# Moving the build of a bias table to the end of the mLSTM, and shorter norm steps for two token blocks, in a two-layer encoder step

## The chip, the cores and the metric

The kernel runs on one core of one Trainium2 chip. The metric is the device time of one execution in microseconds (us), a median over runs. The engines are called as in the profile: PE is TensorE's matrix multiply and PEld its weight load, DVE is VectorE, ACT is ScalarE, POOL is GpSimd, SP is the engine from whose queue nearly all DMAs of this kernel are issued.

## The reference, cut to what matters

The step has two layers over 1024 prompt tokens and 32 sample tokens, 1024 features, all in float32. Layer 0 mixes with an mLSTM, layer 1 with a chunk-band attention that adds a learned bias per head and clipped distance. Each layer ends in a squared-ReLU MLP of width 4096, and each of the four sublayers ends in a LayerNorm.

```python
def trunk(x, ...):
    for l in range(DEPTH):
        sh1, sc1, g1, sh2, sc2, g2 = jnp.split(ada_mod(c, p['w_ada'][l], p['b_ada'][l])[:, None, :], 6, axis=-1)
        u = x * (1 + sc1) + sh1
        ...  # y = mlstm_mixer(u) in layer 0, band attention with rel_bias(table) and @ w_out_b in layer 1
        x = layer_norm(ALPHA * x + (1 + g1) * y, p['ln_g'][l, 0], p['ln_b'][l, 0])
        u = x * (1 + sc2) + sh2
        f = jnp.square(jax.nn.relu(u @ p['w_up'][l])) @ p['w_down'][l]
        x = layer_norm(ALPHA * x + (1 + g2) * f, p['ln_g'][l, 1], p['ln_b'][l, 1])

def rel_bias(table, q_off, tq, tk):            # table: 16 heads x 257 distances
    rel = q_off + jnp.arange(tq)[:, None] - jnp.arange(tk)[None, :]
    idx = jnp.clip(rel, -MAX_REL, MAX_REL) + MAX_REL
    return table[:, idx].astype(jnp.float32)
```

## The kernel before, in words

Features lie on the partitions (8 chunks of 128), tokens along the free axis. The tokens are handled in three blocks, `TBS`: block 0 and block 1 have 384 tokens, block 2 has 288. Every float32 product is three passes of a rounded format (lines 118 to 120: high part times high part, high times low, low times high), so a weight tile is first loaded raw, then rounded to a high part on ACT (line 89) and the rest taken on DVE (line 90). Raw tiles live in a ring of three buffers under the tag `raw`, split weights in a ring of six under the tag `wc`.

The stages come one after the other: mLSTM of layer 0 with its output gates (`o_proj`), its output projection (`op_a`), the up product of layer 0, its down product (`dn_plain`, eight groups g of four weight tiles `w_dn`; the last group goes block by block), the query and key products, the attention, the output projection of layer 1 (`op_b`), and the up and down products of layer 1.

Side work is cut into generators and handed to a `Flow` object. The main loops call `flow.tick(us)`; each tick lowers the waiting time of every task, and a task whose time has run out runs on to its next `yield`, whose value is its next waiting time. So a tick's number places side work between units of matrix work in program order. The framework then orders the instructions of each engine from that program order and its own estimates, before anything runs; on the chip each engine goes through its list in order. Only where `tc.manual_schedule` stands is PE's order taken as written.

Two pieces of side work matter here.

`bias_table` builds in DRAM (`bias_d`, 16 x 64 x 576) the bias that the attention will read: it loads the table (`tab`), turns it on ACT and DVE into one row per head (`rev`), writes that to DRAM (`e_d`), and from there a DMA with a stride of -1 writes the 64 shifted copies. Both tiles, `tab` and `rev`, are taken from the ring `raw`. It is called at the end of `ada_rest`, the task that runs under the down product of layer 0. Its reader is at lines 1784 and 1788, at the start of the attention.

`norm` is the LayerNorm of one token block. Its steps are: the sum over features (`s_n`, split into `sr_n`), a wait `w[0]`, the mean by two matmuls with a matrix of 1/1024 (`mean_n`), the squares (`q_n`, split into `qr_n`), a wait `w[1]`, the variance by two matmuls (`var_n`), then the scaling and the modulated input of the next product (`u`, features in four pairs of chunks with waits `w[2]` to `w[4]` between them), then the gain and shift. In layer 1's output projection the blocks come in the order 2, 1, 0, and `end_out1(ti)` starts the norm of block `ti` when its last feature chunk has been added. One feature chunk of one block, called a unit here, is 24 matmuls, and ends with `flow.tick(n / 96)`, which is 4.0 for a block of 384 tokens.

```python
    W10 = ((10.0, 12.0, 0.0, 0.0, 0.0, 3.0), (16.0, 14.0, 0.0, 0.0, 0.0, 3.0))
    ...
        norms[ti] = flow.add(norm(ti, 2, f"n10_{ti}", W10[ti == rev[-1]], True, ...), now=NOW)
```

With this, blocks 2 and 1 have waits of 10 and 12, block 0 of 16 and 14.

Of the kernel before, what the change touches and what calls it, by code (L numbers as in the profile page):

```python
# [75 lines left out]
def trunk_kernel(ctx: ExitStack, tc: tile.TileContext, a, o):  # L76
    nc = tc.nc
    flow = Flow()
# [5 lines left out]
    def raw_tile(shape, name):  # L84
        return ring.tile(shape, F32, tag="raw", name=name, bufs=3)
# [71 lines left out]
    def lng(i):  # L157
        return pt1[:, i * KC:(i + 1) * KC]

    def lnb(i):  # L160
        return pt1[:, 32 + i * KC:32 + (i + 1) * KC]
# [3 lines left out]
    def ada_part(l, i):  # L165
        return ada[:, l * 48 + i * KC:l * 48 + (i + 1) * KC, :]
# [10 lines left out]
    def tpt(name):  # L177
        return pa.tile([P, 512], F32, tag="tp", name=name, bufs=2)
# [129 lines left out]
    def ada_fix(base, parts):  # L308

        for i, kind in parts:  # L310
            ap = ada[:, base + i * KC:base + (i + 1) * KC, :]
            if kind == "sc":
                nc.vector.tensor_scalar_add(ap, ap, 1.0)
            else:
                nc.vector.tensor_scalar(ap, ap, 1.0, 1.0 / ALPHA, op0=ALU.add, op1=ALU.mult)

    def combine(ni, g, b, sc, sh):

        for cnd in range(2):
            nc.vector.tensor_mul(comb[:, ni, :, 0, cnd], g, sc[:, :, cnd])  # L320
            nc.vector.tensor_mul(comb[:, ni, :, 1, cnd], b, sc[:, :, cnd])
            nc.vector.tensor_add(comb[:, ni, :, 1, cnd], comb[:, ni, :, 1, cnd], sh[:, :, cnd])
# [22 lines left out]

    def bias_table():

        tab = raw_tile([16, 257], "tab")
        nc.sync.dma_start(tab, a["rel_bias_b"][0])
        rev = raw_tile([16, 640], "rev")  # L350
        nc.vector.memset(rev[:, 639:640], 0.0)
        nc.scalar.activation(rev[:, 0:447], tab[:, 256:257].broadcast_to([16, 447]), AF.Copy, scale=8.0)
        fwd = tab[:, 65:257]
        nc.vector.tensor_scalar(rev[:, 447:639], bass.AP(fwd.tensor, fwd.offset + 191, [fwd.ap[0], [-1, 192]]),
                                8.0, None, op0=ALU.mult)
        nc.sync.dma_start(e_d, rev)

        nc.sync.dma_start(bias_d, bass.AP(e_d.tensor, e_d.offset + 63, [[640, 16], [-1, 64], [1, 576]]))


# [28 lines left out]
    def y4_tile(shape, name):  # L389
        return A.tile(shape, F32, tag="y", name=name, bufs=4)  # L390
# [420 lines left out]
    def out_rows():  # L811
        ps = tpt("tails_ps")
        nc.tensor.transpose(ps[:48, :P], tails.rearrange("p j f -> p (j f)"), ident)
        tr = A.tile([P, 256], F32, tag="hn", name="tails_r", bufs=2)[:48, :P]
        nc.vector.tensor_copy(tr, ps[:48, :P])
        nc.sync.dma_start(o["conv_p"].rearrange("l b j (k p) -> (l b j k) p", p=P), tr[0:24])
        nc.sync.dma_start(o["conv_s"].rearrange("l b j (k p) -> (l b j k) p", p=P), tr[24:48])
        ps = tpt("ncol_ps")
        nc.tensor.transpose(ps[:8, :P], ncol, ident)
        nr = A.tile([P, 256], F32, tag="hn", name="ncol_r", bufs=2)[:8, :P]  # L820
        nc.vector.tensor_copy(nr, ps[:8, :P])
        nc.sync.dma_start(o["n_p"][0, 0], nr[0:4])
        nc.sync.dma_start(o["n_s"][0, 0], nr[4:8])
        yield
    flow.add(out_rows())
    units = [0]

    def split_heads(t0, n):
# [39 lines left out]
    def acc_dma(d, x, out=False):  # L868
        for i in range(0, KC, 4):
            p = [d[:, i:i + 4], x[:, i:i + 4]]  # L870
            nc.sync.dma_start(*(p if out else reversed(p)))
# [9 lines left out]
    TAIL = (1.0, 1.5)  # L881
    W00 = (6.0, 12.0, 0.0, 0.0, 0.0, 3.0)
    W01 = ((4.0, 6.0, 1.0, 1.0, 1.0), (6.0, 8.0, 2.0, 2.0, 2.0), (3.0, 6.0, 0.0, 0.0, 0.0))
    W10 = ((10.0, 12.0, 0.0, 0.0, 0.0, 3.0), (16.0, 14.0, 0.0, 0.0, 0.0, 3.0))

    def make_layer(acc, pp, uo, cut=None):

# [654 lines left out]
    fwd, rev = (0, 1, 2), (2, 1, 0)  # L1542
# [10 lines left out]
    mm, norm, _, out_proj, _, add_gated_at = make_layer(acc, bank, uap)  # L1553
    combine(0, lng(0), lnb(0), ada_part(0, 4), ada_part(0, 3))
    norms = {}
# [26 lines left out]
    def ada_rest():  # L1582
        yield from ada_wide(a["w_ada"][1], 0, 48, 48, mm, tmp_t, wc_tile, ADA_W)
        yield from ada_wide(a["w_ada_kv"], D, 104, 8, mm, tmp_t, wc_tile, ADA_W)
        ada_fix(48, [(1, "sc"), (2, "g"), (4, "sc"), (5, "g")])
        ada_fix(96, [(1, "sc")])
        combine(1, lng(1), lnb(1), ada_part(1, 1), ada_part(1, 0))
        combine(2, lng(2), lnb(2), ada_part(1, 4), ada_part(1, 3))
        yield
        bias_table()  # L1590

    class L0:
        wups = wup0
# [41 lines left out]
        def down():  # L1635
            flow.finish(norms["ada"])
            norms["ada"] = flow.add(ada_rest(), carry=True)
# [323 lines left out]
    def open_u2(pr):  # L1961
        u2_cm.append(tc.tile_pool(name=f"u2p{pr}", bufs=1, side="right", reuse_waits="tile"))
        u2p[pr] = u2_cm[-1].__enter__()
        u2[pr] = u2p[pr].tile([P, 2, KC, 2 * QN], F32R, tag="u2", name=f"u2_{pr}")

    def u2ap(hl, k, t0, n):
# [5 lines left out]
    mm, norm, norm_out, out_proj, gain_shift, add_gated_at = make_layer(  # L1972
        acc, lambda name: psD.tile([P, 512], F32, tag="mm", name=name, bufs=8), u2ap, 2 * QN)
# [6 lines left out]

    def end_out1(ti):
        t0, n = TBS[ti]
        norms[ti] = flow.add(norm(ti, 2, f"n10_{ti}", W10[ti == rev[-1]], True, lambda ti: acc_dma(
            xsp[2][:, :, t0:t0 + n], acc[ti], True)), now=NOW)
        qo_cm[ti].__exit__(None, None, None)
        if ti == 1:
            open_u2(0)
# [6 lines left out]
    def early_up(ti, pr):  # L1994

        if ti == rev[-1] and pr:
            wup1[FIRST[pr - 1]] = up_weights(1, FIRST[pr - 1])
    out_proj([(0,), (1, 2, 3)], rev, wo_get, o_mov, ada_part(1, 2), end_out1, "b", width=[384, 384, 320],
             after_pr=early_up)

# [96 lines left out]
```

## Time and profile before

| what | value |
|---|---|
| median of 3 runs | 2437.98 us (2436.84 to 2437.99) |
| the profiled execution | 2433.89 us, of which the span is 2432.1 us |
| mean granted clock of TensorE | 0.993 |
| PE busy | 97% of the span |
| DVE busy | 81% |
| ACT busy | 48% |
| DMA moved | 423.60 MB |

The span is the time from the first to the last instruction of the profiled execution. Rows of a timeline have the start, the duration, the engine, the line and the operation as out<-in; a bracket at the end says how long the engine sat idle before it and what ended that. Rows of a table of stretches have, for each engine, its busy time and number of instructions, then the granted clock of TensorE (1.00 is full), the share of the DMA engines that was busy, and GB/s.

### The profile page before, as it was taken

The page shows a single profiled execution, that of the slowest core. Times are in us where ns is not written, and L with a number is a line of the kernel's source. Part 1 is how long each engine was busy: PE and PEld are TensorE (multiplying, and loading weights), DVE is VectorE, ACT ScalarE, POOL GpSimd, SP SyncE. Part 2 cuts the span into 40 slices and gives each one's busy share as a digit, 9 for nine tenths or more (in the row PEclk, how much of TensorE's full clock was granted, in tenths as well). Part 3 has the DMA queues.
Part 4 walks back from the last instruction along what each step waited for, and adds up shares of the span by engine and source line. Part 5 has one row for each costly group of instructions (what it writes and reads, how often), then busy time and mean ns, then how long its engine had stood idle before and what let it go on. Part 6 is the DMA issues. An engine that isn't in the chain of part 4 may idle for free.

```text
span 2432.1 us, 44293 instructions
## 1 busy us (share of the span) xinstructions
PE 2361.3 (97%) x17180; PEld 2265.0 (93%) x17180; DVE 1973.5 (81%) x4094; ACT 1179.6 (48%) x2394; POOL 166.8 (7%) x315
## 2 busy tenths in 40 slices
PE   7999999999999999999999989999999999899997
PEld 4999999999999999999989977889999999899997
DVE  4898997778788789999697666755998888887778
ACT  4654456377666620010157566763776777222212
POOL 0211100000000000000001134420000000000003
PEclk9999999999999999999999999999999999999999
DMA  8433323436556897656423220051486779966642
GB/s 296 122 112 96 101 88 99 143 114 219 179 188 192 294 346 265 234 203 231 145 67 95 74 64 1 15 135 32 163 282 229 256 259 339 364 243 232 227 151 72
DMA packets 283702, 423.60 MB, mean 174 GB/s; under 512 B 15320, under 2 KB 205164, under 8 KB 278372
## 3 DMA queue, kind: packets, MB, share of 16 engines
q1 hardware_dynamic: 279460, 390.50, 48.1%
q10 hardware_dynamic: 4032, 30.28, 3.1%
q8 instruction: 135, 2.21, 0.4%
q14 instruction: 75, 0.61, 0.1%
HBM read 304.91 MB, written 118.17 MB: 174 GB/s over the span
## 4 chain that ended last, share of the span: by engine, by line
PE 48%; DVE 12%; ACT 4%; DMA 3%; issue 2%; POOL 0%; SPq 0%; DVEq 0%; ACTq 0%; POOLq 0%
PE dn L1421 11%; PE up L1286 8%; PE dn L120 5%; PE dn L119 5%; PE dn L118 5%; PE pv L1859 3%; PE s L1802 2%; PE pt L1837 2%; DVE wf_u L90 1%; DVE HL L90 1%; DMA rdn_u<-in_w_up_dram 1%; PE op_b L118 1%; PE op_b L119 1%; PE op_b L120 1%; PE q L119 1%
## 5 line engine op out<-in xcount | busy, mean ns | idle before, releaser
L1051 DVE SCALAR_TENSOR_TENSOR ACX<-dn,ada,ACX 128x264 f32<-128x264 f32 (+6 forms) x664 | 281.8, 447 | 87.9 <-PE dn L1421 42.5
L1421 PE MATMUL dn<-fx,wf_d 128*128 128x264 f32 x2016 | 255.3, 286 | 6.0 <-DVE ACX L1051 3.7
L1421 PEld LDWEIGHTS dn<-fx,wf_d 128*128 128x128 f32 x2016 | 250.2, 189 | 8.1 <-DVE ACX L1051 2.3
L89 ACT CAST w_dn<-raw_dn 128x1024 fp32r<-128x1024 f32 x36 | 37.7, 1051 | 282.8 <-DVE aw L277 159.5
L118 PE MATMUL dn<-hs,w_dn 128*128 128x384 f32 (+2 forms) x512 | 161.3, 315 | 0.8 <-DVE ACX L1051 0.7
L119 PE MATMUL dn<-hs,w_dn 128*128 128x384 f32 (+2 forms) x512 | 160.9, 315 | 0.0
L120 PE MATMUL dn<-hs,w_dn 128*128 128x384 f32 (+2 forms) x512 | 155.9, 314 | 1.8 <-DVE w_dn L90 1.8
L1286 PE MATMUL up<-TF,wf_u 128*128 128x264 f32 x1056 | 143.4, 285 | 3.0 <-ACT H L1289 3.0
L1286 PE MATMUL up<-U,wf_u 128*128 128x264 f32 x1056 | 139.6, 285 | 1.5 <-DVE H L1292 1.1
L1286 PE MATMUL up<-u,wf_u 128*128 128x264 f32 x1056 | 139.7, 285 | 1.2 <-ACT wf_u L89 0.6
L277 DVE SCALAR_TENSOR_TENSOR aw<-radw,cs,aw 128x512 f32<-128x512 f32 x196 | 139.5, 744 | 0.0
L1286 PEld LDWEIGHTS up<-TF,wf_u 128*128 128x128 f32 x1056 | 134.3, 188 | 4.1 <-ACT H L1289 4.0
L1286 PEld LDWEIGHTS up<-U,wf_u 128*128 128x128 f32 x1056 | 133.0, 188 | 2.6 <-DVE H L1292 1.9
L1286 PEld LDWEIGHTS up<-u,wf_u 128*128 128x128 f32 x1056 | 132.6, 188 | 2.2 <-ACT wf_u L89 0.8
L119 PE MATMUL dn<-U,w_dn 128*128 128x384 f32 (+2 forms) x416 | 129.8, 313 | 0.0
L118 PE MATMUL dn<-U,w_dn 128*128 128x384 f32 (+2 forms) x416 | 129.3, 311 | 0.0
L120 PE MATMUL dn<-U,w_dn 128*128 128x384 f32 (+2 forms) x416 | 125.5, 312 | 0.6 <-DVE w_dn L90 0.6
L120 PEld LDWEIGHTS dn<-hs,w_dn 128*128 128x128 f32 x512 | 95.8, 188 | 2.9 <-DVE w_dn L90 2.6
L118 PEld LDWEIGHTS dn<-hs,w_dn 128*128 128x128 f32 x512 | 96.4, 188 | 1.4 <-DVE ACX L1051 1.0
L119 PEld LDWEIGHTS dn<-hs,w_dn 128*128 128x128 f32 x512 | 96.4, 188 | 0.0
L1812 DVE CUSTOM_DVE_ANT_0 p<-s,bias 128x576 f32<-128x576 f32 (+9 forms) x132 | 79.0, 606 | 19.6 <-PE s L1802 12.8
L90 DVE TENSOR_TENSOR HL<-H,HL 128x1056 fp32r<-128x1056 f32 x64 | 80.2, 1254 | 17.5 <-ACT HL L89 17.4
(394 smaller groups left out, 7163.4 us busy)
## 6 DMA issues: line engine op xcount, KB each, us to landing
hpl<-HL SPq DMA_DIRECT2D x144, 264.0 KB
rdn_u<-in_w_up_dram SPq DMA_DIRECT2D x64, 512.0 KB
hd<-HL SPq DMA_DIRECT2D x28, 1056.0 KB
fx<-hd SPq DMA_DIRECT2D x50, 528.0 KB
radw<-in_w_ada_dram SPq DMA_DIRECT2D x24, 1024.0 KB
hd<-HM SPq DMA_DIRECT2D x28, 792.0 KB
raw_up<-in_w_up_dram SPq DMA_DIRECT2D x40, 512.0 KB
raw_dn<-in_w_down_dram SPq DMA_DIRECT2D x36, 512.0 KB
```

The lines of the kernel that those rows point to most:

```text
L90: (eng or nc.vector).tensor_sub(dst_l, src, dst_h.bitcast(F32))
L118: nc.tensor.matmul(ps, wh, mov(0, k), start=(k == 0), stop=False)
L119: nc.tensor.matmul(ps, wh, mov(1, k), start=False, stop=False)
L120: nc.tensor.matmul(ps, wl, mov(0, k), start=False, stop=(k == nk - 1))
L277: nc.vector.scalar_tensor_tensor(acc[cnd], raw[:, k], sc, acc[cnd], op0=ALU.mult, op1=ALU.add)
L1051: nc.vector.scalar_tensor_tensor(xs, ps[:, off + o:off + o + mm_], gate[:, fc, cnd:cnd + 1], xs, op0=ALU.mult, op1=ALU.add)
L1286: nc.tensor.matmul(p, self.ws[w][:, wl, k], moving(f, tp, xl, k), start=first and k + n_ == 0, stop=k == 3 and n_ == 2, skip_group_check=n ...
L1421: nc.tensor.matmul(p, ws[w][:, wl, k], t[:, s0, xl], start=first and k + n_ == 0, stop=k == kg - 1 and n_ == 2, skip_group_check=not first)
L1802: nc.tensor.matmul(s[:, b, :w], qst, kk[i][:, g, k0 + j0:k0 + j0 + w], start=(i == 0), stop=(i == 1))
L1812: nc.vector.tensor_tensor_reduce(out=z.rearrange("p (b w) -> p b w", b=np_), in0=s[:, :np_, :w], in1=bt.rearrange("p (b w) -> p b w", b=np ...
L1837: nc.tensor.transpose(pt[:kp, j - j0, pr * P:(pr + 1) * P], ps_[pr][:, j * P:j * P + kp], ident)
L1859: nc.tensor.matmul(pv[64 * e:64 * e + 64, :nq], V[:kp, vt0 + j, g * 64:(g + 1) * 64], pts[e][:kp, j, :nq], start=(j == 0), stop=(j == nt - 1))
```

## The change

`bias_table` becomes a generator with one `yield` ahead of its last DMA. Its two tiles come from the tag `y` of the mLSTM's own pool (four buffers) instead of the ring `raw`. It is handed to the flow right behind `out_rows`, at the start of the output gates of heads 2 and 3, the last stage of the mLSTM. The call at the end of `ada_rest` is gone. The waits of the norm in layer 1's output projection get a row for each block: block 0 keeps 16 and 14, block 1 gets 9 and 10, block 2 gets 6 and 8.

```diff
     def bias_table():
-        tab = raw_tile([16, 257], "tab")
+        tab = y4_tile([16, 257], "tab")
         nc.sync.dma_start(tab, a["rel_bias_b"][0])
-        rev = raw_tile([16, 640], "rev")
+        rev = y4_tile([16, 640], "rev")
...
         nc.sync.dma_start(e_d, rev)

+        yield
         nc.sync.dma_start(bias_d, bass.AP(e_d.tensor, e_d.offset + 63, [[640, 16], [-1, 64], [1, 576]]))
...
     flow.add(out_rows())
+    flow.add(bias_table())
...
-    W10 = ((10.0, 12.0, 0.0, 0.0, 0.0, 3.0), (16.0, 14.0, 0.0, 0.0, 0.0, 3.0))
+    W10 = ((16.0, 14.0, 0.0, 0.0, 0.0, 3.0), (9.0, 10.0, 0.0, 0.0, 0.0, 3.0), (6.0, 8.0, 0.0, 0.0, 0.0, 3.0))
...
         combine(2, lng(2), lnb(2), ada_part(1, 4), ada_part(1, 3))
-        yield
-        bias_table()
...
-        norms[ti] = flow.add(norm(ti, 2, f"n10_{ti}", W10[ti == rev[-1]], True, lambda ti: acc_dma(
+        norms[ti] = flow.add(norm(ti, 2, f"n10_{ti}", W10[ti], True, lambda ti: acc_dma(
             xsp[2][:, :, t0:t0 + n], acc[ti], True)), now=NOW)
```

## The prediction

> **What bounds the kernel.** I read the engine rows of the page first, then the table of PE's own waits, then the timeline of PE around the two places that the change touches.
>
> ```profile
> PE 2361.3 (97%) x17180; PEld 2265.0 (93%) x17180; DVE 1973.5 (81%) x4094; ACT 1179.6 (48%) x2394; POOL 166.8 (7%) x315
> PE var_n L929 <- ACT qr_n L89: 6.2, 2, 4.2
> ```
>
> PE is busy 97% of the span, so it sets the time: side work costs or saves only where it makes PE wait. The second row is the largest entry of PE's waits; one wait for a norm's variance is 4.2 us. The whole change can therefore win only what PE loses in such waits. The three that lie where the change works are these:
>
> ```profile
> 1199.05 0.44 PE L118 MATMUL dn<-hs,w_dn 128*128 128x384 f32 x1 [0.71 <-DVE ACX L1051]
> 1203.26 0.45 PE L120 MATMUL dn<-hs,w_dn 128*128 128x384 f32 x1 [1.31 <-DVE w_dn L90]
> 1714.06 0.69 PE L929 MATMUL var_n<-qr_n,ones_d 128*128 128x384 f32 x1 [4.20 <-ACT qr_n L89]
> 1709.86:1714.06 4.20, 0.00 (x1) 0.00 (x0) 3.97 (x6) 1.52 (x3) 0.00 (x0) 1.00 0.41 140
> 1714.06:1716.00 1.94, 1.94 (x7) 1.92 (x8) 1.94 (x4) 0.09 (x1) 0.00 (x0) 0.50 0.90 261
> 1716.00:1718.00 2.00, 2.00 (x13) 2.00 (x12) 1.25 (x2) 1.97 (x4) 0.00 (x0) 0.64 0.76 206
> ```
>
> The last three are rows of the table of stretches. PE does nothing for 4.20 us while DVE is busy 3.97 us of them, so DVE is the late one; and when PE goes on, its granted clock is 0.50 and then 0.64. That is a second price: 1.94 x 0.50 + 2.00 x 0.36 = 1.7 us. The wait costs 4.2 + 1.7 = 5.9 us.
>
> **The bias table leaves the down product.** What it does there:
>
> ```profile
> 1144.27 0.34 SPq L349 DMA_DIRECT2D tab<-in_rel_bias_b_dram  x1
> 1157.03 0.58 ACT L352 ACTIVATE rev<-tab 16x447 f32<-16x447 f32 x1 [12.84 <-DVE w_dn L90]
> 1172.16 0.24 DVE L354 TENSOR_SCALAR rev<-tab 16x192 f32<-16x192 f32 x1
> 1172.47 0.33 SPq L356 DMA_DIRECT2D e_d<-rev  x1
> 1174.20 0.60 SPq L358 DMA_DIRECT2D bias_d<-e_d  x1
> 1174.85 6.89 SPq L96 DMA_DIRECT2D raw_dn<-in_w_down_dram  x3
> ```
>
> Its compute is 0.58 us of ACT and 0.24 us of DVE, which is nothing. But `tab` holds one of three raw buffers from 1144.27 to 1172.4 (28 us) and `rev` a second one for its last part, and SP has to wait for `e_d` to land before it issues `bias_d` at 1174.20. Only behind that are the last three raw tiles of the down weights issued. Their road to PE:
>
> ```profile
> 1189.22 1.05 ACT L89 CAST w_dn<-raw_dn 128x1024 fp32r<-128x1024 f32 x1 [11.67 <-DMA raw_dn<-in_w_down_dram]
> 1201.46 0.62 DVE L1051 SCALAR_TENSOR_TENSOR ACX<-dn,ada,ACX 128x384 f32<-128x384 f32 x1 [2.47 <-PE dn L120]
> 1201.99 3.49 DVE L90 TENSOR_TENSOR w_dn<-raw_dn,w_dn 128x1024 fp32r<-128x1024 f32 x3
> 1180.00:1199.00 19.00, 18.34 (x114) 18.01 (x112) 6.87 (x14) 3.15 (x3) 0.00 (x0) 1.00 0.48 138
> 1204.00:1220.00 16.00, 16.00 (x92) 15.70 (x91) 12.05 (x17) 2.62 (x3) 0.00 (x0) 1.00 0.53 164
> ```
>
> DVE has time: it is busy 6.87 us of the 19 before 1199. The three splits of `w_dn` could run at 1190 to 1194, right behind their casts. They run at 1201.99, because DVE's list, ordered ahead of time, has them behind an addition that PE releases at 1201.46. My reading is that the list was ordered for weights expected late, and that they were expected late because of the two held buffers. With the buffers free the loads can go at about 1144 and 1157, where `tab` and `rev` stood, some 18 to 30 us earlier, and the splits move up in DVE's list. I take both waits as gone: 0.71 + 1.31 = 2.0 us. Bounds: 0 if the list keeps its order, 2.0 if not. No more can come from here: block 0's norm is started by PE's own products, so it moves forward with PE, and the waits behind it stay as they are. The clock behind these two waits is 1.00 (last row), so they have no second price.
>
> **The bias table enters the end of the mLSTM.** The trace shows no such work there, so its cost is bounded by the rows of its new neighbours:
>
> ```profile
> 379.27 0.29 SPq L823 DMA_DIRECT2D out_dram<-ncol_r  x1
> 411.15 2.30 SPq L96 DMA_DIRECT2D raw_oa<-in_w_out_a_dram  x2
> 385.00:400.00 15.00, 15.00 (x88) 15.00 (x87) 7.89 (x15) 9.37 (x21) 0.00 (x0) 1.00 0.01 2
> 378.74 0.49 ACT L454 ACTIVATE og<-o 128x384 f32<-128x384 f32 x1 [1.66 <-PE o L120]
> 382.95 0.49 ACT L454 ACTIVATE og<-o 128x384 f32<-128x384 f32 x1 [1.45 <-PE o L120]
> ```
>
> The task stands behind `out_rows`, whose last DMA is issued at 379.27. SP's queue then has nothing until 411.15, and the DMA engines are 0.01 busy. So SP can wait for `e_d` (1.73 us before, from 1172.47 to 1174.20) with nothing queued behind it, and the 2304 KB of `bias_d` (16 x 64 x 576 x 4 bytes) move in an empty stretch, a thousand us before their reader. The added wait is ACT's and DVE's for `tab` to land; queued behind it are the output gates, which free PE's accumulators. A unit takes 4.21 us (378.74 to 382.95), and three accumulators rotate under the tag `mm`, so PE runs on for two units, 8.4 us, less the time that a unit's gate needs to free one, under 4.21 - 1.45 = 2.8 us, since ACT then sits idle: some 5.6 us of cover. The landing of a small DMA, 1.73 us, is far below. I take 0, with bounds of 0 and +3: a gain is excluded, since work is only added there. The two `y` buffers belong to head 2, which is done.
>
> **The norm steps.** Here is block 2's norm under block 1's units, and then block 1's norm under block 0's units:
>
> ```profile
> 1661.52 0.46 DVE L90 TENSOR_TENSOR sr_n<-s_n,sr_n 128x288 fp32r<-128x288 f32 x1 [0.56 <-ACT sr_n L89]
> 1671.35 0.43 PE L929 MATMUL mean_n<-sr_n,ones_d 128*128 128x288 f32 x2
> 1678.60 0.46 DVE L90 TENSOR_TENSOR qr_n<-q_n,qr_n 128x288 fp32r<-128x288 f32 x1 [0.56 <-ACT qr_n L89]
> 1684.10 0.43 PE L929 MATMUL var_n<-qr_n,ones_d 128*128 128x288 f32 x2
> 1686.20 0.46 DVE L957 SCALAR_TENSOR_TENSOR w_n<-var_n,w_n 128x288 f32<-128x288 f32 x1 [1.28 <-ACT w_n L956]
> 1671.30:1684.10 12.80, 12.80 (x76) 12.80 (x75) 7.43 (x12) 3.09 (x5) 0.00 (x0) 1.00 0.01 1
> 1684.10:1697.00 12.90, 12.90 (x76) 12.90 (x76) 11.24 (x24) 9.48 (x20) 0.00 (x0) 1.00 0.00 1
> 1696.86 0.52 PE L929 MATMUL mean_n<-sr_n,ones_d 128*128 128x384 f32 x2
> 1713.50 0.51 ACT L89 CAST qr_n<-q_n 128x384 fp32r<-128x384 f32 x1 [2.63 <-DVE q_n L949]
> ```
>
> Between block 2's mean and its variance lie three units, so one is (1684.10 - 1671.35 - 0.43) / 3 = 4.1 us; it lowers a waiting time by 4.0. Block 1's waits of 10 and 12 are three units each, and its new 9 and 10 are three units each too: that edit changes nothing. Block 2's go from three and three units to two and two (6 and 8). So its mean comes at 1671.35 - 4.1 = 1667.2; its sum is ready at 1662.0, so PE doesn't wait. Its variance comes two units later, at 1667.2 + 0.43 + 8.2 = 1675.8. From mean to split squares the chain took 1679.06 - 1671.35 = 7.7 us, so they are ready at 1674.9, with 0.9 us to spare. Everything behind the variance starts 8.3 us earlier, at 1677.9 instead of 1686.20, in a stretch where DVE is busy 7.43 of 12.8 us. Today part of it sits on block 1's path. The first row is DVE's time on `ut_n`, block 2's modulated input, from block 1's mean to its split squares; the second is DVE's and ACT's time on `w_n`, block 2's scale, in the stretch before. Both are rows of the table of stretches, cut to one tile. Then come the groups of up weight splits in that stretch and of the adds in block 1's sum, and a wait further on:
>
> ```profile
> 1696.86:1714.52 17.66, 4.87 (x16) 0.00 (x0) 0.99 0.43 131
> 1684.10:1696.86 12.76, 3.40 (x6) 1.39 (x3) 1.00 0.00 1
> L90 DVE TENSOR_TENSOR w_up<-raw_up,w_up 128x1024 fp32r<-128x1024 f32 x4 | 4.9, 1218 | 0.0
> L934 DVE TENSOR_TENSOR s_n<-s_n,ACC 128x768 f32<-128x768 f32 x2 | 1.9, 948 | 0.0
> 1791.66 0.39 PE L120 MATMUL up<-u,w_up 128*128 128x264 f32 x1 [1.10 <-DVE w_up L90]
> ```
>
> Of 17.7 us on block 1's chain, DVE spends 4.87 on block 2. PE wanted the squares at 1709.86; their high part came at 1713.50 + 0.51 = 1714.0. If the 4.87 us have been worked off before, it comes at 1709.1, and the wait is gone. Whether all of them have: from 1677.9 to 1696.86 DVE has 19.0 us. Block 2's second half is 24 instructions on `ut_n`, 7.3 us at 4.87 for 16, and seven on `w_n`, 4.0 at 3.40 for six: 11.3. Block 1's sum is three adds at 0.95 and two of half their size, some 4.0; five additions of units at 0.62 (the row at 1201.46) are 3.1. That is 18.4 us. It just fits, so the last of the four pairs of chunks, about 2.6 us, may still fall into block 1's chain; then 4.2 - (4.87 - 2.6) = 1.9 us of wait stay. I take the middle, 0.9 us, for the range 0 to 1.9.
>
> What a remaining wait costs beyond itself is read from another place, where PE waited 1.67 us:
>
> ```profile
> 2075.57 1.69 PE L1421 MATMUL dn<-fx,wf_d 128*128 128x264 f32 x7 [1.67 <-DVE ACX L1051]
> 2075.50:2077.50 2.00, 1.93 (x10) 1.94 (x10) 2.00 (x7) 0.85 (x1) 0.00 (x0) 0.59 1.10 435
> ```
>
> After 1.67 us the granted clock was 0.59; after the 1.31 us at 1203 it wasn't lowered. So I let 0.9 cost nothing more, and 1.9 the 1.7 us again. The Trainium skill ("TensorE: Matmul & The Clock Gate", the section on why this matters for your kernels) says that only gaps of more than about 3 us between bursts are to be avoided; the row at 2075 speaks against it. By that rule a remaining 1.9 us would cost only itself, and the norm part would come to -4.0 instead of -2.3 us.
>
> Behind it, the wait of 1.10 us on `w_up` at 1791.66 hangs on DVE's list too; DVE gets ahead by about as much as PE, so this wait stays or shrinks (0 to -1.1). PE being the bound, I take what is won as kept to the end.
>
> **The sum.** -2.0 (down weights) + 0 (new place) - 4.2 - 1.7 + 0.9 (variance) = -7.0 us. Against the profiled execution, 2433.89 (span 2432.1 and 1.8 around it), that is 2426.9. The runs' median, 2437.98, lies 4.1 us above that execution, so the forecast for a median is 2431.0.
>
> **Rivals.** (1) *The weight splits take block 2's place.* The four splits of `w_up` are 4.9 us in that same stretch, and no part of the change moves them. If they, or block 2's last pair, are drawn closer to the front of DVE's list, 1.9 us of wait and the lowered clock stay: -2.0 - 2.3 = -4.3, so 2433.7. For it: the fit above is tight. Against it: DVE's list before block 1's mean has them anyway behind the sum.
>
> (2) *The down weights don't move*, or the freed buffers only draw the query weights forward and a split of those stands in the way: the norm alone, -5.0, so 2433.0. For it: my reading of why the splits stand late is inferred from the order, no row shows an expected time. Against it: 28 us of a held buffer.
>
> (3) *Block 2's variance comes too early, and it is slower.* Its squares have 0.9 us to spare. If DVE's list puts other work into that chain (weight splits, the bigger sums), PE stands, and block 2's second half is late again. At the length that block 1's chain has, 17.7 us, PE would wait 17.7 - 8.6 = 9.1 us, with 1.7 for the clock, and block 1's wait would stay: -2.0 + 10.8 = +8.8, so 2446.8. With a wait of w the second half still starts 8.3 - w earlier, so the norm part's 5.0 shrinks in proportion: w + 1.7 - 2.0 - 5.0 x (1 - w / 8.3) turns positive at w = 3.3, a chain of 12 us. Against it: DVE is half empty there, ACT 3.09 busy of 12.8, and DMA 0.01, so nothing else is ready.
>
> (4) *Nothing is moved that counts*: the framework orders the lists anew and both stalls come back elsewhere: 2438.
>
> **How the numbers follow.** Forecast 0.50, (1) 0.22, (2) 0.12, (3) 0.10, (4) 0.06. About 0.2%, 4.9 us, is what a measurement of this kernel can tell from no change, so faster means below 2433.1. That holds for nearly all of the forecast's half, and for part of (1) and (2), which lie at the border: 0.58. The rest of those two and (4) give 0.31 for the same, and (3) with a small share of (4) 0.11 for slower. The forecast's own range is 2429.0 (-2.0 - 5.9 - 1.1 with the up weights' wait) to 2433.0. The whole range, 2428.0 to 2438.0, leaves out (3) and the edges.
>
> **What would show it.** Right: no idle of PE near 1199 and 1203; the last raw down tiles issued before 1170 and their splits before 1195; block 2's variance one mean and two units after its mean with no wait; the row of block 1's variance with an idle under 1.9 us and a granted clock of 1.00 behind it; `bias_d` moving between 380 and 400 with PE busy 15.00 of 15. Wrong: an idle before block 2's variance, block 1's variance still late by over 2 us, a new wait for query weights near 1205 to 1250, or output gates of heads 2 and 3 that wait for `rev`.

## The result, and the profile after

| | before | after |
|---|---|---|
| median of the runs | 2437.59 us | 2442.28 us |
| the profiled execution (span) | 2433.89 (2432.1) us | 2442.15 (2440.0) us |
| mean granted clock | 0.993 | 0.991 |

The ratio is 1.0018, with a 95% interval from 1.0011 to 1.0024: slower by 4.7 us, where 2431.0 with a range of 2428 to 2438 had been forecast. Of the changed kernel's page the engine row, and two rows of PE's own waits (total, number, longest):

```profile
PE 2364.5 (97%) x17180; PEld 2268.4 (93%) x17180; DVE 1978.0 (81%) x4094; ACT 1180.0 (48%) x2394; POOL 165.6 (7%) x315
PE adas L299 <- DVE cx L288: 6.6, 1, 6.6
...
PE op_a L118 <- ACT w_oa L89: 3.5, 1, 3.5
```

The variance of a norm has left the table, where it stood at the top with 6.2 us. Two entries are new that nothing in the forecast named: `adas`, a sum of the layer 0 modulation, which now heads the table, and `op_a`, the output projection of layer 0. The timeline of PE has them within 21 us of each other; below them stand the rows that answer to the query stage and to the norm of layer 1 (line 931 is norm, line 299 modulation):

```profile
431.29 0.44 PE L118 MATMUL op_a<-U,w_oa 128*128 128x384 f32 x1 [3.53 <-ACT w_oa L89]
451.85 0.31 PE L299 MATMUL adas<-cx,sel 128*32 128x16 f32 x8 [6.55 <-DVE cx L288]
...
1262.00 0.45 PE L931 MATMUL mean_n<-sr_n,ones_d 128*128 128x384 f32 x1 [0.53 <-ACT sr_n L89]
1271.51 0.49 PE L120 MATMUL q<-U,w_q 128*128 128x384 f32 x1 [2.74 <-DVE w_q L90]
1278.95 0.42 PE L118 MATMUL q<-U,w_q 128*128 128x384 f32 x1 [1.74 <-DVE QO L1683]
...
1682.07 0.43 PE L931 MATMUL mean_n<-sr_n,ones_d 128*128 128x288 f32 x2
1690.66 0.43 PE L931 MATMUL var_n<-qr_n,ones_d 128*128 128x288 f32 x2
1711.74 0.52 PE L931 MATMUL mean_n<-sr_n,ones_d 128*128 128x384 f32 x2
1724.58 0.52 PE L931 MATMUL var_n<-qr_n,ones_d 128*128 128x384 f32 x2
```

The table of stretches gives what the clock adds (the column before the last two is the granted clock):

```profile
431.29:433.30 2.01, 2.01 (x7) 1.75 (x8) 1.60 (x3) 0.00 (x0) 0.00 (x0) 0.70 1.04 401
433.30:435.30 2.00, 2.00 (x8) 2.00 (x7) 1.53 (x4) 0.00 (x0) 0.00 (x0) 0.50 1.06 385
451.85:454.00 2.15, 2.02 (x13) 1.92 (x14) 2.12 (x5) 1.10 (x2) 0.00 (x0) 0.50 0.69 230
454.00:456.00 2.00, 2.00 (x8) 2.00 (x8) 1.66 (x2) 1.04 (x1) 0.00 (x0) 0.50 0.48 117
```

New losses: 3.53 + 6.55 us of waiting, and 2.01 x 0.30 + 2.00 x 0.50 = 1.6 and 4.15 x 0.50 = 2.1 us of lowered clock, 13.8 us in all. Won: block 1's 4.2 + 1.7 = 5.9 us. Between 1190 and 1295 PE's waits of over 0.5 us sum to 7.1 us before (six entries) and to 0.53 + 2.74 + 1.74 = 5.0 us after: 2.1 us. The lowered clock behind these waits cancels: about 1.7 us before (0.87, 0.50 and 0.78 in the three stretches of 2 us from 1262) and 1.7 us after (the rows at 1271.50 and 1273.50 in the last section). 13.8 - 5.9 - 2.1 = +5.8 us, between the 4.7 us of the runs and the 8.3 us of the two profiled executions. Part of the 8.3 us isn't the change's: a `cu` matmul of the mLSTM that starts at 167.37 before starts at 169.06 after, ahead of all that was moved, and in the other profiled runs anywhere between 167.43 (e6) and 172.42 (e8).

So both places from which a gain was forecast gave it, and the third, priced at 0 to +3, cost some 14 us. SP's queue shows where that begins. In it `raw_o` are weights of the output gates, in buffers of the ring `raw`, and `ada_room` is the one buffer through which the weights of the layer 0 modulation come. Before:

```profile
305.38 0.38 SPq L96 DMA_DIRECT2D raw_o<-in_w_in_a_dram  x1
310.32 0.38 SPq L261 DMA_DIRECT2D ada_room<-in_w_ada_dram  x1
311.80 0.37 SPq L96 DMA_DIRECT2D raw_o<-in_w_in_a_dram  x1
325.02 24.16 SPq L261 DMA_DIRECT2D ada_room<-in_w_ada_dram  x2
355.38 6.46 SPq L96 DMA_DIRECT2D raw_o<-in_w_in_a_dram  x2
...
428.54 0.37 SPq L261 DMA_DIRECT2D ada_room<-in_w_ada_dram  x1
```

After, and with it the largest entry of SP's own waits in this stretch:

```profile
290.36 0.46 SPq L349 DMA_DIRECT2D tab<-in_rel_bias_b_dram  x1
...
297.30 0.45 SPq L356 DMA_DIRECT2D e_d<-rev  x1
...
303.63 0.83 SPq L359 DMA_DIRECT2D bias_d<-e_d  x1
312.18 0.40 SPq L261 DMA_DIRECT2D ada_room<-in_w_ada_dram  x1
312.67 44.17 SPq L96 DMA_DIRECT2D raw_o<-in_w_in_a_dram  x2
...
438.65 0.38 SPq L261 DMA_DIRECT2D ada_room<-in_w_ada_dram  x1
```

```profile
SPq L96 <- PE S L661: 43.7, 1, 43.7
```

The table isn't built behind `out_rows` (374 us) but at 290. My reading is that its two `y` buffers are free by then and that the framework lists an instruction as soon as it can run; e6 and e8 below, where the table moves with the time at which its tile comes free, fit that. Behind the copy the order is another one: both `raw_o` loads stand ahead of the next `ada_room` load. The second of them has to wait for a raw buffer until 356 (44.17 us from the first issue to the end of the second), and SP stands, with the modulation's loads behind it. The buffer in question holds `cl`, a state of head 3, which is loaded at 289.85 and read by PE for the last time at 356.2, just ahead of the `S` that the row names. In between DVE, which has the modulation's sums, and the DMA engines have less to do than before (rows of the tables of stretches, before and after):

```profile
320.00:350.00 30.00, 30.00 (x172) 28.16 (x172) 27.72 (x90) 14.83 (x44) 2.36 (x5) 1.00 0.11 37
```

```profile
320.00:350.00 30.00, 30.00 (x175) 28.96 (x175) 21.02 (x74) 15.60 (x44) 2.29 (x5) 1.00 0.00 1
```

6.7 us of DVE's work are missing from these 30 us alone; they fall due later. The changed kernel's copy has landed by then: the DMA engines are 0.70 busy from 315 to 320 and 0.00 from 320 to 330. The last load of the modulation goes at 438.65 instead of 428.54, and its sums run at 443.94 instead of 435.48, on DVE (the first fence is before, the second after):

```profile
435.48 5.39 DVE L277 SCALAR_TENSOR_TENSOR ada_acc<-ada_room,cs,ada_acc 128x512 f32<-128x512 f32 x8 [0.74 <-DMA ada_room<-in_w_ada_dram]
```

```profile
443.94 5.39 DVE L277 SCALAR_TENSOR_TENSOR ada_acc<-ada_room,cs,ada_acc 128x512 f32<-128x512 f32 x8 [3.74 <-DMA ada_room<-in_w_ada_dram]
```

`adas` stands in PE's list at a fixed place and waits for them. The wait of `op_a` is the same thing 20 us earlier. DVE's list has six sums of the modulation ahead of the last splits of `U`, and ACT casts the weight only when those splits are done (rows of DVE, then of ACT, after):

```profile
421.80 4.06 DVE L277 SCALAR_TENSOR_TENSOR ada_acc<-ada_room,cs,ada_acc 128x512 f32<-128x512 f32 x6
...
428.23 1.93 DVE L90 TENSOR_TENSOR U<-G,U 128x288 fp32r<-128x288 f32 x5
430.19 1.04 ACT L89 CAST w_oa<-raw_oa 128x1024 fp32r<-128x1024 f32 x1 [7.61 <-DVE U L90]
```

Before, the last split of `U` runs at 422.43, and the cast behind it sits idle for 0.53 us.

### The profile page after: what moved, and what is told of

It reads as the page before. It is cut to its first block, busy times and chain, and to the rows that moved or that the text cites. A ratio compares the mean times of both kernels' runs of the same rounds, so it can differ in the third digit from the quotient of the medians.

```text
span 2440.0 us, 44311 instructions
## 1 busy us (share of the span) xinstructions
PE 2364.5 (97%) x17180; PEld 2268.4 (93%) x17180; DVE 1978.0 (81%) x4094; ACT 1180.0 (48%) x2394; POOL 165.6 (7%) x315
## 4 chain that ended last, share of the span: by engine, by line
PE 48%; DVE 11%; ACT 4%; DMA 4%; issue 2%; POOL 1%; SPq 0%; ACTq 0%; DVEq 0%; POOLq 0%
PE dn L1423 11%; PE up L1288 9%; PE dn L120 5%; PE dn L119 5%; PE dn L118 4%; PE pv L1859 3%; PE s L1802 2%; PE pt L1837 2%; PE op_b L118 1%; PE op_b L119 1%; PE op_b L120 1%; DVE wf_u L90 1%; DMA rdn_u<-in_w_up_dram 1%; DVE HL L90 1%; PE q L120 1%
```

## The experiments

All ratios are to the kernel before on the same chip, with 95% intervals; its median there was 2434.6 (e1 to e8) and 2435.0 us (e9 to e12). The theory: the norm steps and the freed raw buffers win what was forecast, and the loss is the order on SP's queue behind the early copy. The rivals were the copy's traffic, the table's own work and its landing waits, and that the norm edit is worth nothing.

**One half each.** e1 is the kernel before with the new rows of `W10`, e2 the changed kernel with the old ones, e12 has the old ones and the table out of the down product and of the ring `raw`, at a later place than the changed kernel's.

```diff
# e1: on the kernel before
-        norms[ti] = flow.add(norm(ti, 2, f"n10_{ti}", W10[ti == rev[-1]], True, ...
+        norms[ti] = flow.add(norm(ti, 2, f"n10_{ti}", W10[ti], True, ...
# e2: on the changed kernel, the reverse of it
# e12: as e8 below, with the old rows of W10
```

> The kernel before with nothing changed but the three rows of norm waits (block 1: 9 and 10, block 2: 6 and 8). Theory A (the norm steps win what was forecast, the loss comes from the bias table's new place): block 1's variance no longer waits 4.2 us and the clock stays up behind it, the two waits for down weights stay: 5 us under the kernel before, ratio 0.998. Rival B (the norm edit moves the waits on to the query weights, and is worth nothing): within 1 us of the kernel before.

Measured: 2426.78 us, ratio 0.9969 (0.9958 to 0.9981), 7.8 us faster. Block 1's wait is gone, PE is busy 30.00 of 30 us where it was 25.80, at a clock of 1.00 instead of 0.94 (1700 to 1730). A stands, B falls. The forecast's 5.0 lies inside the interval (4.6 to 10.2).

> The changed kernel with the old norm waits; only the bias table is moved. Theory A: the two PE waits at the end of the mLSTM and in the output projection (3.5 and 6.6 us, each with a lowered clock behind it) are there again, the down weights' 2.0 us are won, block 1's variance waits 4.2 us again: about 10 us over the kernel before, ratio 1.004. Rival B: the same as the changed kernel, 4.7 us over before.

Measured: 2445.86 us, ratio 1.0048 (1.0035 to 1.0060), 11.3 us slower, with PE waits of 6.4 us on `adas`, 3.4 on `op_a` and 4.1 on `var_n`. The halves add up: -7.8 + 11.3 = +3.5, against +4.7 for both.

> The kernel with the table in the up phase, but with the old norm waits: the freed raw buffers alone. By the prediction's step: the two PE waits of 0.71 and 1.31 us near 1199 and 1203 gone, 2 us under the kernel before, ratio 0.9992. Rival (the wait only moves on to the query weights): within 1 us of before, ratio 1.000.

Measured: 2432.84 us, ratio 0.9990 (0.9981 to 0.9999), 2.2 us faster. PE's two waits for `w_dn` are gone, as in the changed kernel. So taking the table out of the down product is worth about the forecast's 2.0 us, though the interval is not far from nothing.

**The traffic or the order?** e3 keeps the order of SP's queue and takes seven eighths of the copy's bytes away; only two heads' bias is written, and the attention reads the first head's for all sixteen.

```diff
-        nc.sync.dma_start(bias_d, bass.AP(e_d.tensor, e_d.offset + 63, [[640, 16], [-1, 64], [1, 576]]))
+        nc.sync.dma_start(bias_d[0:2], bass.AP(e_d.tensor, e_d.offset + 63, [[640, 2], [-1, 64], [1, 576]]))
```

> The changed kernel, but the copy into the bias buffer moves 2 of the 16 heads (288 KB instead of 2304 KB) and the readers take those heads' bias for all; everything else stands in the same order on every queue. Theory A1 (the order on SP's queue is the cause: the loads of the layer 0 modulation stand behind a weight load that cannot be issued until 356 us): no change from the changed kernel, 4.7 us over before, waits of 3.5 and 6.6 us still there. Rival A2 (the copy's traffic delays the loads behind it): the two waits shrink or go, 2432 to 2435 us.

Measured: 2437.42 us, ratio 1.0013 (1.0005 to 1.0022), within the interval of the changed kernel; the two waits are 6.0 and 3.4 us. From 305 to 310 the DMA engines are 0.13 busy, where the changed kernel has 0.96. The traffic is not the cause.

**Another queue.** e4 issues the copy from ACT's queue.

```diff
-        nc.sync.dma_start(bias_d, ...)
+        nc.scalar.dma_start(bias_d, ...)
```

> The changed kernel, but the copy into the bias buffer is issued from ACT's queue instead of SP's. The framework then orders SP's queue differently: five loads of the layer 0 modulation stand ahead of the output gate weights of head 2. Theory A1: the modulation is done long before the out projection, the two PE waits are gone, and the forecast's gain appears: 7 us under the kernel before (2431 us), plus up to 3 us if ACT stands at the copy until its source has landed. Rival A3 (the early table's own work, its landing waits on ACT and DVE inside the mLSTM, is what costs): still 3 to 5 us over the kernel before.

Measured: 2474.97 us, ratio 1.0172 (1.0158 to 1.0186), 40 us slower. Neither theory had that. SP's queue and PE's timeline of e4:

```profile
310.61 48.63 SPq L261 DMA_DIRECT2D ada_room<-in_w_ada_dram  x5
366.79 9.12 SPq L96 DMA_DIRECT2D raw_o<-in_w_in_a_dram  x2
```

```profile
335.60 0.31 PE L299 MATMUL adas<-cx,sel 128*32 128x16 f32 x8 [19.24 <-DVE cx L288]
366.82 0.69 PE L120 MATMUL o<-U,w_o 128*128 128x384 f32 x1 [25.70 <-DVE w_o L90]
```

The order has tipped over to the other side: five modulation loads stand ahead of head 2's output gate weights, PE's list has `adas` at 335.60 instead of 416.7, and PE waits 19.24 us for the modulation and 25.70 us for the weight. That weight had been loaded at 289.46; its split stands behind the modulation's sums in DVE's list too (365.55). The expectation had the right order and the wrong consequence: here it costs more to be early with the modulation than to be late. The Trainium skill ("DMA: Bandwidth & Descriptors", "Issuing engines are not separate DMA queues") says that DMAs of all issuing engines end up on the same 16 DMA engines. By that a change of queue alone should give next to nothing; the 40 us of e4 are waits that come from the order of the lists, and no run here changes the queue alone.

**The early work without the copy, and the place that was meant.** e5 is the kernel before with the new rows of `W10`; it keeps the old table complete and adds a second early one, without its copy. e6 has the changed kernel's table in the tile that is only free when head 3 has read its decay rows; `tab` is loaded at 351.35 there.

```diff
# e5: added behind out_rows; early_table is bias_table in y buffers up to its write, into a second DRAM buffer
+    flow.add(early_table())
# e6
-        tab = y4_tile([16, 257], "tab")
-        rev = y4_tile([16, 640], "rev")
+        both = rc_tile([16, 1024], "tab")
+        tab = both[:, 0:257]
+        rev = both[:, 320:960]
```

> The old bias table stays where it was and complete; with the new norm waits. Added behind out_rows is a second, early table (its load, ACT's and DVE's work, its row per head written to a second DRAM buffer), but no copy out of it. Theory A1 (it is the copy's place on SP's queue, behind the wait for its source, by which the loads of the layer 0 modulation fall behind): the queue keeps the order of the kernel before, no PE waits of 3 and 6 us at 430 to 452; as fast as the norm steps alone, ratio 0.997, 2427 us. Rival A3 (the early table's own landing waits, on ACT, DVE and SP): 3 us or more above that, waits in the out projection.

Measured: 2429.21 us, ratio 0.9980 (0.9972 to 0.9989), 5.4 us faster; no waits at 430 to 452. It is 2.4 us above e1, with intervals that overlap; a small cost of the early work isn't excluded here, but e9 below has the same work and no such loss.

> The changed kernel, but tab and rev lie in the one tile that holds the mLSTM's decay rows until head 3 has read them for the last time, so that the table cannot be built before about 355 us: it stands where the prediction had put it. Theory A1: this place costs nothing or up to 3 us, the modulation is in time; the norm steps' 7.8 and the down weights' 2 us appear: 2425 us, ratio 0.996. Rival A4 (any copy on SP's queue in the mLSTM or the output gates makes the modulation late): waits of 3 to 7 us of PE in the out projection again, 2435 us or more.

Measured: 2439.59 us, ratio 1.0025 (1.0016 to 1.0033), 5.0 us slower. A1 falls as worded; A4 holds for the time, though the larger waits are in the output gates and not in the out projection. Queue and PE of e6:

```profile
355.41 0.38 SPq L96 DMA_DIRECT2D raw_o<-in_w_in_a_dram  x1
356.73 0.60 SPq L360 DMA_DIRECT2D bias_d<-e_d  x1
370.43 1.79 SPq L727 DMA_DIRECT2D out_dram<-co  x2
372.27 0.46 SPq L96 DMA_DIRECT2D raw_o<-in_w_in_a_dram  x1
```

```profile
389.77 0.44 PE L120 MATMUL o<-U,w_o 128*128 128x384 f32 x1 [1.95 <-DVE w_o L90]
397.89 0.69 PE L118 MATMUL o<-U,w_o 128*128 128x384 f32 x1 [4.16 <-DVE og L459]
```

Near the place where the prediction had put it, the table costs too: the last output gate weight goes 11 us later than before (372.27 against 361.5, the second of the two loads at 355.38), PE waits 1.95 and 4.16 us in the output gates, and 2.08 and 1.76 us later on. SP stands at the copy for about a microsecond; the weight is late by its place in the list, now behind the stores of a head's state, which SP can't issue before 370.43. That it is the copy that moved it there isn't shown: no run has this place without the copy.

**The copy's length.** e9 leaves 8 of the 1024 rows, still on SP, still behind the wait for `e_d`; the attention reads one row for all. e10 leaves the rows and takes the wait away: it copies from `rev` in SBUF.

```diff
# e9
+        nc.sync.dma_start(bias_d[0:2, 0:4], bass.AP(e_d.tensor, e_d.offset + 63, [[640, 2], [-1, 4], [1, 576]]))
# e10
-        nc.sync.dma_start(e_d, rev)
+        nc.sync.dma_start(bias_d, bass.AP(rev.tensor, rev.offset + 63, [rev.ap[0], [-1, 64], [1, 576]]))
```

> The changed kernel, but the early copy moves 8 rows of the 1024 (18 KB instead of 2304 KB), and the readers take row 0 of head 0 for all; the copy still stands on SP's queue behind the wait for its source. With 128 rows (the run before) the order of SP's queue was the same as with 1024; with 8 rows the framework puts the loads of the layer 0 modulation back among the output gate weights. Theory A5 (the framework expects the copy to take long, and plans the modulation late; on the chip only that order costs): the PE waits of 3.5 and 6.6 us are gone, 2427 us, ratio 0.997. Rival A6 (the table's work or SP's wait for the source, in itself): still over 2435 us.

Measured: 2423.72 us, ratio 0.9953 (0.9939 to 0.9967), 11.3 us faster, and 16 us below the changed kernel by the two differences (+4.7 and -11.3). SP's queue of e9 has the modulation between the output gate weights again:

```profile
303.52 0.69 SPq L359 DMA_DIRECT2D bias_d<-e_d  x1
307.13 0.38 SPq L96 DMA_DIRECT2D raw_o<-in_w_in_a_dram  x1
312.06 0.37 SPq L261 DMA_DIRECT2D ada_room<-in_w_ada_dram  x1
313.53 0.37 SPq L96 DMA_DIRECT2D raw_o<-in_w_in_a_dram  x1
326.75 24.01 SPq L261 DMA_DIRECT2D ada_room<-in_w_ada_dram  x2
```

> The changed kernel, but the copy reads rev from SBUF, so that the write to DRAM and SP's wait for it fall away; the 1024 rows stay, at the same early place. Theory A5 (the copy's planned length moves the modulation): SP's queue still has modulation loads behind weight loads that cannot be issued until about 356 us, and PE still waits several us in the out projection: over 2433 us, between the kernel before and the changed one. Rival A7 (SP's wait for the source is what moves it): 2427 us, no waits of 3 us there.

Measured: 2457.31 us, ratio 1.0085 (1.0072 to 1.0099), 22 us slower, more than expected, with waits of 10.1 us on `adas` and 7.1 on `op_a`. In its queue the two `raw_o` loads stand together again, and take longer:

```profile
313.11 56.73 SPq L96 DMA_DIRECT2D raw_o<-in_w_in_a_dram  x2
```

A7 falls, and with e9 A6. The order follows the size of the copy: 8 rows leave it, 128 and 1024 rows move it. That the framework expects a long transfer there is the reading that fits all four kernels; its expected times stand in no trace. The size of e10's loss is not all order: from 305 to 324 the DMA engines are 0.89 busy and more at only some 100 GB/s, which I read as the copy straight from SBUF, and from 320 to 330 they are 0.87 busy where the changed kernel has 0.00. How much of the 22 us that makes isn't separated.

```profile
320.00:330.00 10.00, 9.85 (x56) 9.75 (x57) 3.85 (x17) 4.46 (x12) 0.46 (x1) 1.00 0.87 216
```

**A version that beats both.** All three have the new rows of `W10`. e7 builds the table at its old place in tiles of the ring of temporaries; e8 and e11 build it when those open, among the up weights' loads, e11 with the copy from SBUF.

```diff
# e7 (bias_table at the end of ada_rest, as before)
-        tab = raw_tile([16, 257], "tab")
+        tab = tmp_t([16, 257], "tab")
-        rev = raw_tile([16, 640], "rev")
+        rev = tmp_t([16, 640], "rev")
# e8, e11: the same tiles, and
-    flow.add(bias_table())          # behind out_rows
     ADA_B = (4.0, 2.0, 1.0, 8.0)
+    flow.add(bias_table())          # ahead of ADA_B
```

> The kernel before with the new norm waits, and the bias table built at its old place, but in tiles of the ring of temporaries, so that it holds no raw buffer. Theory of the prediction (the two held raw buffers made the down weights late): the PE waits of 0.71 and 1.31 us near 1199 and 1203 are gone, 2 us under the norm steps alone, 2425 us. Rival (SP's wait for the table's rows is what made them late): the waits stay, 2427 us.

Measured: 2431.47 us, ratio 0.9988 (0.9980 to 0.9997), 3.1 us faster, but 4.7 us above e1 (the two intervals just meet). The wait of 0.71 us is gone, that on `w_dn` is still there (1.32 us, at 1214.79), and a norm of the query stage waits longer:

```profile
1264.43 0.69 PE L929 MATMUL var_n<-qr_n,ones_d 128*128 128x384 f32 x1 [6.57 <-ACT qr_n L89]
```

There the copy stands between the last down weights (1173.99, the weights at 1173.42 and 1175.08), and the lists behind it have come out differently again: free buffers alone are not the gain. Neither the theory nor the rival is borne out as worded.

> The changed kernel, but tab and rev are temporaries of the pool that opens when the mLSTM's has been closed, so that the table is built about 440 us, among the loads of the up weights. Theory A1: nothing before 430 us differs from the kernel before, so no PE waits of 3 us and more there; with the norm steps and the freed raw buffers 2425 us, ratio 0.996; against it stand up weights that are loaded up to 3 us later.

Measured: 2427.19 us, ratio 0.9971 (0.9960 to 0.9982), 7.4 us faster, no wait before 460 us that the kernel before hasn't. Against the changed kernel's 1.0018 the copy's place is worth 0.47%, 11.5 us.

> The kernel with the table in the up phase (temporaries, new norm waits), with the copy taken from SBUF directly: one DMA and one wait less on SP's queue. Expected: as the table in the up phase, 2427 us, or up to 1 us less, ratio 0.997; a rival is that the copy, one load earlier among the up weights, makes those late: PE waits for w_up, 1 to 3 us more.

Measured: 2424.87 us, ratio 0.9952 (0.9938 to 0.9966), 10.2 us faster than before: the norm steps, the table out of the down product, and a place where the copy's order costs nothing that shows. It is the best complete kernel here; whether the direct copy itself gives anything over e8 stays open, since the two intervals overlap.

## Why the prediction was wrong, step by step

- **The down weights** (-2.0): right in size, partly right in way. The changed kernel runs some 16 us late there, by its own matmuls, so its times are read less 16 us. Two raw tiles are issued at 1161.55 and 1174.30, that is at 1145.5 and 1158, where 1144 and 1157 were forecast. The splits run at 1192.78 to 1197.69, that is ahead of 1195 as forecast, and the two waits are gone (`w_dn` keeps 2.3 us in the table of PE's waits by an early wait of 1.30 us at 915, which is 0.32 us in e1 and 1.01 in e8). The last raw tile goes at 1192.28, that is at 1176, some 5 us earlier than before but not ahead of 1170. The query weights behind have waits of 2.74 and 1.74 us, where there were 1.32, 2.04, 0.86 and 0.91 before. The stage as a whole saves 2.1 us, and e12 2.2. But e7 frees the same buffers, leaves the copy in the stage, and keeps one of the two waits: the held buffers were not the only reason.
- **The norm steps** (-5.0): right in mechanism, and in size within the interval of e1, 7.8 us (4.6 to 10.2). Block 2's variance follows its mean by two units, 1690.66 - 1682.07 - 0.43 = 8.2 us, with no wait; (9, 10) is three units and three. Block 1's chain, from its mean to its split squares, had 17.2 us and has 11.0 (1711.74 to 1722.7), where 4.87 us of relief were allowed; so none of the 0.9 us for a remaining wait is left.
- **The bias table's new place** (0, bounds 0 to +3): this is the step that failed. The first sentence of it, that the task stands behind `out_rows`, whose last DMA is issued at 379.27, takes program order for the queue's order. The prediction itself says that DVE's list is "ordered ahead of time", and used that for the down weights; here it priced only what the added instructions do on the chip (landing, bytes, waits), and for those 0 was right as far as the runs can tell: e9 has the added instructions and waits without the bytes and loses nothing, and with seven eighths of the bytes gone e3 is no faster than the intervals allow for chance. The price was what the copy does to the list: 11.5 us (e8), 14 us (the trace) or 16 us (e9), far above the bound of +3. In e6, with the table near the place that was expected, the kernel is slower too.
- **The rivals**: the first three were about the norm and the down weights. Rival (4) had the lists ordered anew, but with both stalls coming back, and they didn't; rival (3) was slower, for another reason. What happened, another task's loads falling behind on SP's queue, was not among them: the queue was read from 379 us on, and the loads that fell behind stand from 310 to 356.

## What to carry to other kernels

Where a framework orders the queues, a moved DMA is not priced by what it transfers or waits for: ask which queue it enters, at what moment it can first run, and whose loads are behind it. Program order doesn't say when that is: here the table ran some 80 us ahead of the task that it was written behind. If the queue has loads that wait for a ring's buffers (44 us here), the order of two neighbours on it can be worth more than the whole transfer. Taking the tile from a pool that opens late helped: it kept the work from being listed early, and took the cost of this move from some 12 us to nothing that these runs can tell.

## What was not expected of the hardware

The granted clock after a wait of PE, rows of the table of stretches of the changed kernel behind the waits of 2.74, 1.74 and (at 2084) 1.46 us:

```profile
1271.50:1273.50 2.00, 1.99 (x7) 1.99 (x8) 2.00 (x4) 0.51 (x1) 0.00 (x0) 0.57 0.40 89
1273.50:1275.50 2.00, 2.00 (x9) 2.00 (x8) 2.00 (x4) 0.27 (x1) 0.00 (x0) 0.58 0.82 253
...
1278.95:1281.00 2.05, 2.05 (x12) 1.86 (x13) 1.86 (x5) 1.55 (x4) 0.00 (x0) 1.00 0.04 12
2084.50:2087.00 2.50, 2.04 (x14) 1.83 (x15) 2.50 (x7) 0.85 (x1) 0.00 (x0) 1.00 1.08 387
```

2.74 us of waiting lowered the clock to 0.57 for about 4 us; 1.74 and 1.46 us didn't, while 1.67 us in the kernel before did (0.59). The cost behind 2.74, 3.53 and 6.55 us is nearly the same: 1.7 (2.00 x 0.43 + 2.00 x 0.42), 1.6 and 2.1 us. So in these rows it is an event with a price, not a price by length, and between 1.4 and 1.8 us the length alone doesn't decide. The Trainium skill ("TensorE: Matmul & The Clock Gate", the section on why this matters for your kernels) sets the limit at about 3 us; the row at 1271 is below it and was slowed.
